# Feed-forward weight parts in three tiles by the order of their products, a fourth load buffer, and the order of loads in the merge

## The chip, the core and the metric

The kernel runs on one core of one Trainium2 chip. A core has TensorE (PE, matrix products), VectorE (DVE), ScalarE (ACT), GpSimd (POOL) and SyncE (SP), which here only issues transfers. The engines run their own instruction streams in order and wait for one another on semaphores. The metric is the device time of one execution in microseconds; the runs give a median.

## The reference, cut to what matters

Two layers of one trunk work on 512 latent and 128 context tokens of width 1024 (640 columns, called T). Each layer is: normalize, three token mixers A, B, C beside each other, a gated sum of their projections (the merge), one output projection, a residual add, normalize, a SwiGLU feed-forward part (FFN) of inner width 2816, a residual add.

```python
merged = g_a * (ya @ p['w_pa']) + g_b * (yb @ p['w_pb']) + g_c * (yc @ p['w_pc'])
...
mix, new_ctx = mixer_block(h, p, ctx, angs)          # returns merged @ p['w_out']
x = x + g1 * mix
h = rms_norm(x, p['norm2']) * (1 + sc2) + sh2
x = x + g2 * ((jax.nn.silu(h @ p['w_gate']) * (h @ p['w_up'])) @ p['w_down'])
```

## The kernel before

**Precision and layout.** Activations lie with features on the 128 partitions and tokens along the columns. A weight is loaded in f32 and split into two f16 tiles, a high part by ACT and a low part by DVE (`split`, L190; for other weights `wload`, L179). A product is then three f16 matmuls per row block of 128 (`mm3`): high by high, low by high, high by low, over 320 columns at a time.

**Who sets the order.** The program is written in data-flow order, and a scheduler puts the instructions of each engine into one static order. Blocks under `high_priority` are preferred, so loads move ahead as far as their buffers allow. A pool with `bufs=n` gives a tile's name n buffers in turn; an instruction that needs one waits for the last user of the old content. Everything that SP issues, gate tiles, branch weights, w_out, FFN weights, residual tiles (x) and modulation weights (wm), stands in one queue. `after` adds an ordering edge between two instructions of one engine without a semaphore.

**The merge** (`merge`, L1129). For each of eight feature blocks m it loads three tiles into `t3` (name mgt, three buffers): the gates of the branches (`d_gate`) or, where a branch was already projected and gated earlier, that result (`d_br`). With the branch weights (`w_br`, one product for m = 0 and two for each other m, each in two halves of 320 columns) PE fills PSUM (six banks, name g), DVE multiplies by the gate (mgt, L1149), POOL adds (mga), and ACT and DVE split the sum into mgh and mgl. Then w_out is loaded in eight blocks of 512 KB through two raw buffers (wf) and split into the eight buffers of the pool wo; three passes over the columns (320, 192, 128) make the output projection, the residual add and the sums of squares.

**The FFN** (`ffn`, L1266). Its three matrices are multiplied by a seven-product scheme on 2 x 2 blocks (Winograd's form of Strassen's). `norm_sums` makes the seven right-hand sides xs. `lhs` (L1201) makes the seven left-hand sides of a weight block: SP loads five sub-blocks of 256 columns into a tile wg (three buffers), POOL's queue adds a sixth onto two of them with an accumulating transfer, ACT and DVE split the three plain sub-blocks (`pw`, 768 columns), DVE adds one sum (L1212), POOL adds another (L1213), and ACT and DVE split the four sums (1024 columns). The seven results lie in one pair of tiles, pw0 and pw1, with five buffers; AT7 says where each product finds its part. `block` runs the products of a block in the order 1, 2, then 6, 5, 7, then 4, 3, and `run` interleaves them so that the 1, 2 of a block stand ahead of the 4, 3 of the block before. Intermediate products go from PSUM to SBUF by ACT copies (dp1, du2, du3, two buffers each). A block of the gate and up matrices has two calls of `lhs`, one of the down matrix one or two; there are 136 calls in the program. In layer 0 the FFN also computes the modulation of layer 1 (wm loads, products into at).

**Memory.** The scratch pool tmp (name sq, for squares) is open for the whole program.

Of the kernel before, what the change touches and what calls it, by code (L numbers as in the profile page):

```python
# [21 lines left out]
KD = 8  # L22
# [106 lines left out]

AT7 = {4: 0, 2: 1, 1: 2, 3: 3, 6: 4, 7: 5, 5: 6}  # L130

BT7 = {1: 0, 2: 1, 3: 2, 5: 3, 7: 4, 4: 5, 6: 6}
WGB = 3
PWB = 5


class Trunk:
    def __init__(self, tc, nc, a, o, ctx, dbg=None):
        self.tc, self.nc, self.a, self.o, self.dbg = tc, nc, a, o, dbg
        pool = lambda n, b, **k: ctx.enter_context(tc.tile_pool(name=n, bufs=b, **k))  # L140
        self.cp = pool("const", 1)
        self.tp = pool("tmp", 2)
        self.ctx = ctx
        self.xpool = None
        self.pspools, self.psn = ExitStack(), 0
        self.last_tanh = self.pending = None
        self.open_psum(at=2, md=1, g=4)
        self.dp = pool("scr", 1, space=DRAM)

    def pool(self, es, name, bufs=1, side=None):  # L150
        return es.enter_context(self.tc.tile_pool(name=name, bufs=bufs, side=side, reuse_waits="tile"))

    def open_x(self):
# [24 lines left out]

    def wload(self, src, n, pool=None, raw=None):  # L179
        nc = self.nc  # L180
        wf = self.sb(raw, [128, n], "wf") if raw else self.sb(self.wp, [128, n], "wf")
        wh = self.sb(pool or self.wq, [128, n], "wh", F16)
        wl = self.sb(pool or self.wq, [128, n], "wl", F16)
        with self.tc.high_priority():
            nc.sync.dma_start(wf, src)
            nc.scalar.activation(wh, wf, AF.Copy, scale=SW)  # L186
            nc.vector.scalar_tensor_tensor(wl, wf, SW, wh, op0=ALU.mult, op1=ALU.subtract)  # L187
        return wh, wl
# [35 lines left out]
    def after(self, i, j):  # L224

        info = mybir.DependencyInfo(mybir.DependencyClass.NoSync, mybir.DependencyReason.DATA)
        self.tc.add_manual_dep(i, j.name, info, reason="function tables")

# [900 lines left out]
    def merge(self, l, mp, wo, wr, mt, ys):  # L1129
        nc = self.nc  # L1130
        mgh = self.sb(mp, [128, KD, T], "mgh", F16)
        mgl = self.sb(mp, [128, KD, T], "mgl", F16)
        for m in range(KD):
            acc = self.sb(mp, [128, T], "mga", bufs=2)
            t3 = self.sb(mt, [128, 3, T], "mgt")
            late = [b for b in (0, 2, 1) if b == 1 or m >= EARLY[b // 2]]
            with self.tc.high_priority():
                for b in range(3):
                    nc.sync.dma_start(t3[:, b], self.d_gate[m, b] if b in late else self.d_br[m, b // 2])
                if late == [1]:  # L1140
                    nc.gpsimd.tensor_tensor(acc, t3[:, 0], t3[:, 2], op=ALU.add)
# [18 lines left out]
        for m in range(KD):  # L1160
            nc.sync.dma_start(self.x[:, m, :], self.xsrc[:, m, :])
            ws.append(self.wload(self.a["w_out"][l, m].rearrange("p k m -> p (k m)"), 1024, wo))
        for x0, x1 in COLS:
# [37 lines left out]
    def lhs(self, pool, src, n):  # L1201
# [4 lines left out]
        with self.tc.high_priority():  # L1206
            a = tile("wg", WGB, F32, 5)
            out = [tile(f"pw{i}", PWB, F16, 7) for i in range(2)]
            nc.sync.dma_start(a, src[:, 0:5])
            nc.gpsimd.dma_start(a[:, 3:5], src[:, 5:6].to_broadcast([128, 2, 128 * n]), accum_op=ALU.add)  # L1210
            self.split(out[0][:, 0:3], out[1][:, 0:3], a[:, 0:3], SW)
            nc.vector.tensor_tensor(a[:, 2], a[:, 4], a[:, 2], op=ALU.add)  # L1212
            nc.gpsimd.tensor_tensor(a[:, 1], a[:, 2], a[:, 1], op=ALU.add)  # L1213
            self.split(out[0][:, 3:7], out[1][:, 3:7], a[:, 1:5], SW)
        return {q: [[out[i][:, j, 128 * k:128 * k + 128] for k in range(n)] for i in range(2)] for q, j in AT7.items()}

    def block(self, pool, chunks, rhs, dst, done, urgent=False, after=None):
# [18 lines left out]

        def copy(p, tag):
            with first():
                t = self.sb(pool, [128, HT], tag, bufs=2)
                self.act(t, p, AF.Copy)  # L1240
                return t
        bank = lambda: self.psum("s")[:, :HT]
        a, b = bank(), bank()
        product(a, 1)
        p1 = copy(a, "dp1")
        product(b, 2)
        add(p1, b, 0)
        yield
        product(a, 6, True)
        u2 = copy(a, "du2")  # L1250
        b = bank()
        product(b, 5)
        product(a, 7, True)
        u3 = copy(a, "du3")
        add(u3, b, 3)
# [10 lines left out]
    def ffn(self, l, fs, ns):  # L1266
# [5 lines left out]
        ns.close()  # L1272
        wp = self.pool(fs, f"fw{l}")
        self.open_psum(s=7, at=1)
        d_x = self.sb(self.dp, [128, KD, T], f"d_x{l}")
# [142 lines left out]
    def layer(self, l):  # L1418
        tc = self.tc
        ys, ws, wfs = ExitStack(), ExitStack(), ExitStack()  # L1420
        self.yh, self.yl = [], []
        self.wp = self.pool(wfs, f"wf{l}", 2)
        self.wq = self.pool(ws, f"wst{l}", 3)
# [98 lines left out]
        with ExitStack() as es:  # L1522
            gp = self.pool(es, f"mg{l}")
            wo, mt = self.pool(es, f"wo{l}", 8), self.pool(es, f"mt{l}", MTB)
            self.merge(l, gp, wo, wr, mt, ys)
        wfs.close()
        with ExitStack() as es:
            self.ffn(l, es, ExitStack())
# [8 lines left out]
def layout(inp):  # L1537
# [45 lines left out]

    six = lambda w: np.stack([w[..., i, j, :, :] for i, j in ((1, 1), (0, 1), (0, 0), (0, 0), (1, 1), (1, 0))], -3)
    r["w_gu"] = six(gu).reshape(L, NF // 2, 2, 2, 128, 6, 256)
# [37 lines left out]
```

## Time and profile before

| | |
|---|---|
| median of 3 runs | 2754.21 us (2751.93 to 2755.40) |
| the profiled execution: its time, its span | 2747.09 us, 2745.2 us |
| PE busy | 2503.0 us (91%) |
| DVE busy | 1739.1 us (63%) |
| ACT busy | 1308.2 us (48%) |
| POOL busy | 941.4 us (34%) |
| mean granted clock of PE | 0.973 |
| moved by transfers | 434.44 MB |

The shares are means over stages with different limits. The stages are found in the timeline: the merge of layer 0 runs from 791.3 to 870.9 us, its output projection from there to about 925, its FFN from 939.1 to 1397.2; in layer 1 the merge begins at 2149.4 and the FFN lasts from 2297.6 to 2732.4.

### The profile page before, as it was taken

To read this page: it belongs to the slowest core of one execution; us is meant where nothing else is said; L and a number is where in the kernel's file an instruction comes from. 1 tells how busy PE (TensorE), PEld (TensorE's weight loads), DVE (VectorE), ACT (ScalarE), POOL (GpSimd) and SP (SyncE) were. 2 spreads that over 40 slices of the span, in tenths; PEclk is the share of its full clock that TensorE was granted. 3 is DMA by queue.
4 is the path that set the end of the run, shared out by engine and by line. 5 is a ranking of instruction groups with operands and counts; after the bars stand their busy time and mean duration, and the time that the engine had idled before them with its cause. 6 is when DMAs were issued, how large, how long until landed. Compare 5 with 4: busy or idle time off the path is not lost.

```text
span 2745.2 us, 53163 instructions
## 1 busy us (share of the span) xinstructions
PE 2503.0 (91%) x21022; PEld 1606.3 (59%) x21022; DVE 1739.1 (63%) x2984; ACT 1308.2 (48%) x2482; POOL 941.4 (34%) x876
## 2 busy tenths in 40 slices
PE   6999999999978899999889989999989788889896
PEld 3656666566336655656666666665753466566664
DVE  5639854325756677677787497432267657676877
ACT  5532754444642544344465345544545425444445
POOL 3252211211126355354433632022012455544544
PEclk9999999999999999999999999999999999999999
DMA  7787564436346187765543965534462641556563
GB/s 293 221 256 233 151 191 124 125 124 204 108 156 183 32 257 217 195 181 135 131 142 109 262 182 163 149 115 120 131 210 74 212 127 30 131 137 153 120 151 100
DMA packets 286395, 434.44 MB, mean 158 GB/s; under 512 B 112000, under 2 KB 192960, under 8 KB 286144
## 3 DMA queue, kind: packets, MB, share of 16 engines
q1 hardware_dynamic: 249152, 396.42, 46.5%
q0 software_dynamic: 36992, 34.61, 8.8%
q8 instruction: 165, 2.70, 0.4%
q14 instruction: 86, 0.70, 0.1%
HBM read 343.21 MB, written 73.92 MB: 152 GB/s over the span
## 4 chain that ended last, share of the span: by engine, by line
PE 44%; DVE 19%; DMA 18%; issue 6%; ACT 6%; POOL 5%; SPq 2%; POOLq 0%; DVEq 0%; ACTq 0%
PE f L199 11%; PE s L199 9%; PE g L199 7%; DMA wg<-in_w_gu 6%; PE ao L876 4%; DVE pw L193 4%; DMA wg<-in_w_down 2%; DVE z L675 2%; ACT pw L192 1%; DVE wl L187 1%; DVE zw L673 1%; POOL wg L1213 1%; DMA d_s<-sd 1%; DVE wg L1212 1%; PE at L980 1%
## 5 line engine op out<-in xcount | busy, mean ns | idle before, releaser
L199 PEld LDWEIGHTS <-pw 128*128 128x128 f16 x5544 | 539.7, 99 | 347.3 <-issue 55.5
L199 PEld LDWEIGHTS <-wh 128*128 128x128 f16 x4944 | 477.6, 99 | 211.5 <-issue 29.7
L199 PE MATMUL s<-xs,pw 128*128 128x320 f16 x3696 | 541.2, 304 | 47.2 <-ACT pw L192 13.3
L192 ACT ACTIVATE pw<-wg 128x1024 f16<-128x1024 f32 (+3 forms) x272 | 247.7, 923 | 251.4 <-POOL wg L1213 157.7
L193 DVE SCALAR_TENSOR_TENSOR pw<-wg,pw 128x1024 f16<-128x1024 f32 (+3 forms) x272 | 314.8, 1171 | 72.8 <-ACT pw L192 71.9
L199 PEld LDWEIGHTS <-wl 128*128 128x128 f16 x2472 | 244.5, 99 | 165.5 <-issue 76.3
L199 PE MATMUL s<-f,pw 128*128 128x320 f16 x1848 | 273.6, 303 | 35.6 <-ACT pw L192 17.1
L199 PE MATMUL f<-hh,wh 128*128 128x320 f16 x896 | 249.5, 300 | 0.1
L199 PE MATMUL f<-hh,wl 128*128 128x320 f16 x896 | 249.5, 300 | 0.0
L879 POOL TENSOR_TENSOR pacc<-pe,pacc 128x512 f32<-128x512 f32 x64 | 84.9, 1327 | 350.6 <-ACT pe L217 317.8
L199 PE MATMUL g<-hh,wh 128*128 128x320 f16 x704 | 201.7, 308 | 3.1 <-ACT sq L217 1.5
L199 PE MATMUL g<-hh,wl 128*128 128x320 f16 x704 | 201.5, 307 | 0.0
L1210 POOL DMA_DIRECT2D wg<-in_w_gu x88 | 105.6, 1205 | 218.9 <-DMA wg<-in_w_gu 120.3
L333 DVE SCALAR_TENSOR_TENSOR wl<-wf,wh 128x512 f16<-128x512 f32 x130 | 90.1, 720 | 142.7 <-ACT wh L217 142.6
L187 DVE SCALAR_TENSOR_TENSOR wl<-wf,wh 128x1024 f16<-128x1024 f32 (+4 forms) x116 | 126.7, 1097 | 36.9 <-ACT wh L186 36.6
L1213 POOL TENSOR_TENSOR wg<-wg 128x256 f32<-128x256 f32 (+1 forms) x136 | 125.0, 924 | 66.2 <-DVE wg L1212 63.8
L199 PE MATMUL f<-hl,wh 128*128 128x320 f16 x896 | 147.3, 299 | 0.0
L1212 DVE TENSOR_TENSOR wg<-wg 128x256 f32<-128x256 f32 (+1 forms) x136 | 91.8, 680 | 87.6 <-DMA wg<-in_w_gu 61.5
L186 ACT ACTIVATE wh<-wf 128x1024 f16<-128x1024 f32 (+4 forms) x116 | 96.0, 833 | 77.3 <-PE g L199 59.1
L217 ACT ACTIVATE pe<-at 128x512 f32<-128x512 f32 x128 | 75.1, 595 | 106.1 <-PE at L981 58.8
L818 POOL TENSOR_TENSOR rc<-rc,rot 128x512 f32<-128x512 f32 (+1 forms) x16 | 30.0, 1872 | 273.3 <-DVE rc L817 183.6
L199 PE MATMUL g<-hl,wh 128*128 128x320 f16 x704 | 114.6, 300 | 0.0
(370 smaller groups left out, 4805.3 us busy)
## 6 DMA issues: line engine op xcount, KB each, us to landing
wg<-in_w_gu SPq DMA_DIRECT2D x88, 640.0 KB, 4.9
wm<-in_w_mod SPq DMA_DIRECT2D x96, 512.0 KB, 5.3
wf<-in_w_in SPq DMA_DIRECT2D x112, 256.0 KB, 3.4
wg<-in_w_down SPq DMA_DIRECT2D x40, 640.0 KB, 4.1
wf<-in_w_in SPq DMA_DIRECT2D x44, 512.0 KB, 3.8
wg<-in_w_gu POOLq DMA_DIRECT2D x88, 256.0 KB, 4.6
d_s<-sd SPq DMA_DIRECT2D x20, 768.0 KB, 5.4
d_gate<-st SPq DMA_DIRECT2D x96, 160.0 KB, 2.7
```

Source lines behind the costliest of these rows:

```text
L186: nc.scalar.activation(wh, wf, AF.Copy, scale=SW)
L187: nc.vector.scalar_tensor_tensor(wl, wf, SW, wh, op0=ALU.mult, op1=ALU.subtract)
L192: nc.scalar.activation(hi, src, AF.Copy, scale=scale)
L193: nc.vector.scalar_tensor_tensor(lo, src, scale, hi, op0=ALU.mult, op1=ALU.subtract)
L199: mm = lambda *a, **k: nc.tensor.matmul(out, *a, skip_group_check=more, **k)
L217: i = self.nc.scalar.activation(out, in_, func, scale=scale, **kw)
L333: nc.vector.scalar_tensor_tensor(wl[:, sl], wf, SW, wh[:, sl], op0=ALU.mult, op1=ALU.subtract)
L876: nc.tensor.matmul(po[64 * j:64 * j + 64, :], vt(h, kt), es[j], start=n == 0, stop=n == 4)
L879: nc.gpsimd.tensor_tensor(acc[1], es[1], acc[1], op=ALU.add)
L1210: nc.gpsimd.dma_start(a[:, 3:5], src[:, 5:6].to_broadcast([128, 2, 128 * n]), accum_op=ALU.add)
L1212: nc.vector.tensor_tensor(a[:, 2], a[:, 4], a[:, 2], op=ALU.add)
L1213: nc.gpsimd.tensor_tensor(a[:, 1], a[:, 2], a[:, 1], op=ALU.add)
```

## The change

- **Order of loads in the merge.** `merge` keeps the last gate load of each m in `lds`. The w_out load of block m is ordered behind the gate loads of step m + 1 (the last two behind those of the last step), and the first four wg loads of the FFN behind the last gate load.
- **Weight parts in three tiles.** The sub-blocks are stored in another order (`six` and AT7), so that the accumulating transfer adds onto a[2:4]. Three pairs of tiles take the split parts: two sub-blocks (products 1 and 2), then, after DVE's sum, the three of products 6, 5 and 7, then, after POOL's sum, those of products 3 and 4. They have four, five and six buffers (PWB), in all as many bytes as before.
- **Buffers.** wg has four buffers. The copies dp1, du2 and du3 share one name with four buffers. tmp is closed before the FFN and opened anew in the next layer; the FFN has a pool of its own for sq.

```diff
-AT7 = {4: 0, 2: 1, 1: 2, 3: 3, 6: 4, 7: 5, 5: 6}
+AT7 = {2: (0, 0), 1: (0, 1), 6: (1, 0), 7: (1, 1), 5: (1, 2), 3: (2, 0), 4: (2, 1)}
...
-WGB = 3
-PWB = 5
+WGB = 4
+PWB = (4, 5, 6)
...
+    def open_tmp(self, l):
+        self.tp = self.pool(self.tmps, f"tmp{l}", 2)
...
-    def wload(self, src, n, pool=None, raw=None):
+    def wload(self, src, n, pool=None, raw=None, behind=None):
...
-            nc.sync.dma_start(wf, src)
+            ld = nc.sync.dma_start(wf, src)
+            if behind is not None:
+                self.after(ld.ins, behind)
...
+        lds = []
         for m in range(KD):
...
                 for b in range(3):
-                    nc.sync.dma_start(t3[:, b], self.d_gate[m, b] if b in late else self.d_br[m, b // 2])
+                    ld = nc.sync.dma_start(t3[:, b], self.d_gate[m, b] if b in late else self.d_br[m, b // 2])
+                lds.append(ld.ins)
...
-            ws.append(self.wload(self.a["w_out"][l, m].rearrange("p k m -> p (k m)"), 1024, wo))
+            ws.append(self.wload(self.a["w_out"][l, m].rearrange("p k m -> p (k m)"), 1024, wo, behind=lds[min(m + 1, KD - 1)]))
+        self.late = [lds[-1]] * WGB
...
             a = tile("wg", WGB, F32, 5)
-            out = [tile(f"pw{i}", PWB, F16, 7) for i in range(2)]
-            nc.sync.dma_start(a, src[:, 0:5])
-            nc.gpsimd.dma_start(a[:, 3:5], src[:, 5:6].to_broadcast([128, 2, 128 * n]), accum_op=ALU.add)
-            self.split(out[0][:, 0:3], out[1][:, 0:3], a[:, 0:3], SW)
-            nc.vector.tensor_tensor(a[:, 2], a[:, 4], a[:, 2], op=ALU.add)
-            nc.gpsimd.tensor_tensor(a[:, 1], a[:, 2], a[:, 1], op=ALU.add)
-            self.split(out[0][:, 3:7], out[1][:, 3:7], a[:, 1:5], SW)
+            ld = nc.sync.dma_start(a, src[:, 0:5])
+            if self.late:
+                self.after(ld.ins, self.late.pop())
+            nc.gpsimd.dma_start(a[:, 2:4], src[:, 5:6].to_broadcast([128, 2, 128 * n]), accum_op=ALU.add)
+            out = []
+
+            def parts(j, x):
+                out.append([tile(f"pw{j}{i}", PWB[j], F16, x.shape[1]) for i in range(2)])
+                self.split(out[j][0], out[j][1], x, SW)
+            parts(0, a[:, 0:2])
+            nc.vector.tensor_tensor(a[:, 1], a[:, 3], a[:, 1], op=ALU.add)
+            parts(1, a[:, 1:4])
+            nc.gpsimd.tensor_tensor(a[:, 0], a[:, 1], a[:, 0], op=ALU.add)
+            parts(2, a[:, 0:5:4])
...
-                t = self.sb(pool, [128, HT], tag, bufs=2)
+                t = self.sb(pool, [128, HT], "du", bufs=4)
...
         wp = self.pool(fs, f"fw{l}")
+        self.tp = self.pool(fs, f"sq{l}", 2)
...
+        if l:
+            self.open_tmp(l)
...
         wfs.close()
+        self.tmps.close()
...
-    six = lambda w: np.stack([w[..., i, j, :, :] for i, j in ((1, 1), (0, 1), (0, 0), (0, 0), (1, 1), (1, 0))], -3)
+    six = lambda w: np.stack([w[..., i, j, :, :] for i, j in ((0, 1), (0, 0), (0, 0), (1, 1), (1, 1), (1, 0))], -3)
```

## Rows read from the trace of the kernel before

**Rows 1.** Windows: stretch, us, busy us (count) of each engine, clock, DMA share, GB/s.

```profile
791.30:870.90 79.60, 58.13 (x398) 39.65 (x397) 58.80 (x74) 27.88 (x39) 47.95 (x44) 0.91 0.86 261
806.80:820.50 13.70, 5.27 (x20) 2.90 (x20) 8.80 (x15) 4.53 (x5) 3.50 (x3) 0.50 1.05 297
870.90:925.00 54.10, 50.75 (x553) 43.78 (x553) 23.68 (x45) 21.71 (x50) 20.23 (x30) 1.00 0.06 21
939.10:1397.20 458.10, 424.53 (x3112) 273.35 (x3111) 333.87 (x503) 204.47 (x330) 210.11 (x206) 0.98 0.67 178
992.00:1070.00 78.00, 72.06 (x569) 42.88 (x568) 55.03 (x71) 33.15 (x54) 41.42 (x40) 1.00 0.85 247
1223.30:1226.70 3.40, 3.40 (x15) 1.91 (x14) 2.76 (x5) 1.52 (x3) 0.86 (x1) 0.50 0.48 119
2297.60:2732.40 434.80, 391.97 (x2729) 266.56 (x2728) 320.57 (x476) 205.85 (x329) 209.28 (x206) 0.98 0.53 123
```

**Rows 2.** PE's waits in 785:872, layer 0's merge: us in total, times, longest.

```profile
PE g L199 <- DVE mgt L1149: 16.8, 7, 12.6
```

**Rows 3.** PE's waits in 2130:2240, layer 1's merge.

```profile
PE g L199 <- DVE mgt L1149: 17.4, 8, 12.4
```

**Rows 4.** Timeline of PE: start, us, engine, line, operation, [idle before, releaser].

```profile
815.23 0.42 PE L199 MATMUL g<-yh,wh 128*128 128x320 f16 x1 [12.58 <-DVE mgt L1149]
```

**Rows 5.** Timeline of SP, which issues the loads, in layer 0's merge.

```profile
796.17 0.37 SPq L1209 DMA_DIRECT2D wg<-in_w_gu  x1
...
799.51 1.59 SPq L185 DMA_DIRECT2D wf<-in_w_out  x2
801.14 4.17 SPq L1139 DMA_DIRECT2D mgt<-d_gate  x4
```

**Rows 6.** PE's waits in 940:1397, layer 0's feed-forward part.

```profile
PE s L199 <- ACT pw L192: 11.8, 10, 2.2
PE s L199 <- DVE pw L193: 7.7, 7, 3.3
PE s L199 <- ACT du L217: 5.7, 5, 3.6
```

**Rows 7.** PE's waits in 2298:2732, layer 1's feed-forward part.

```profile
PE s L199 <- ACT pw L192: 18.6, 18, 2.9
PE s L199 <- DVE pw L193: 12.4, 19, 1.6
```

**Rows 8.** The page's groups: count, busy us, mean ns, idle before, releasers.

```profile
L199 PE MATMUL s<-xs,pw 128*128 128x320 f16 x3696 | 541.2, 304 | 47.2 <-ACT pw L192 13.3
```

**Rows 9.** The page's DMA issues: count, KB each, us to landing.

```profile
wg<-in_w_gu SPq DMA_DIRECT2D x88, 640.0 KB, 4.9
...
wg<-in_w_gu POOLq DMA_DIRECT2D x88, 256.0 KB, 4.6
```

**Rows 10.** Timeline of SP in 990:1075: first and eleventh weight block.

```profile
992.02 0.33 SPq L1209 DMA_DIRECT2D wg<-in_w_gu  x1
...
1069.77 0.33 SPq L1209 DMA_DIRECT2D wg<-in_w_down  x1
```

**Rows 11.** Forms in 1000:1395 on DVE, on ACT; tile pw (min/median/max ns).

```profile
L193 DVE SCALAR_TENSOR_TENSOR pw<-wg,pw 128x1024 f16<-128x1024 f32 x53 | 69.4, 1315 | 23.3 <-ACT pw L192 23.0
L193 DVE SCALAR_TENSOR_TENSOR pw<-wg,pw 128x768 f16<-128x768 f32 x53 | 53.2, 1026 | 2.5 <-ACT pw L192 2.4
...
L193 DVE SCALAR_TENSOR_TENSOR pw<-wg,pw 128x512 f16<-128x512 f32 x4 | 3.7, 914 | 2.5 <-ACT pw L192 2.5
...
L192 ACT ACTIVATE pw<-wg 128x1024 f16<-128x1024 f32 x53 | 55.6, 1053 | 69.4 <-POOL wg L1213 69.0
...
L192 ACT ACTIVATE pw<-wg 128x512 f16<-128x512 f32 x4 | 2.5, 626 | 4.5 <-POOL wg L1213 4.5
...
L193 DVE SCALAR_TENSOR_TENSOR pw<-wg,pw x272: 546/1210/3508, 803.6 to 2720.3; 128x768 f16<-128x768 f32 x62, 128x1024 f16<-128x1024 f32 x62, 128x384 f16<-128x384 f32 x8, 128x512 f16<-128x512 f32 x4
```

**Rows 12.** SP's waits in 785:940.

```profile
SPq L304 <- DVE nts L1195: 73.2, 2, 71.3
```

More of the change, by code (lines that the diff above doesn't have):

```diff
@@ L141, in __init__ @@
         self.cp = pool("const", 1)
-        self.tp = pool("tmp", 2)
         self.ctx = ctx
+        self.tmps = ExitStack()
+        self.open_tmp(0)
         self.xpool = None
@@ L226, in after @@
         info = mybir.DependencyInfo(mybir.DependencyClass.NoSync, mybir.DependencyReason.DATA)
-        self.tc.add_manual_dep(i, j.name, info, reason="function tables")
+        self.tc.add_manual_dep(i, j.name, info, reason="order")
     def load_ln_exp(self):
@@ L1207, in lhs @@
             a = tile("wg", WGB, F32, 5)
-            out = [tile(f"pw{i}", PWB, F16, 7) for i in range(2)]
-            nc.sync.dma_start(a, src[:, 0:5])
-            nc.gpsimd.dma_start(a[:, 3:5], src[:, 5:6].to_broadcast([128, 2, 128 * n]), accum_op=ALU.add)
-            self.split(out[0][:, 0:3], out[1][:, 0:3], a[:, 0:3], SW)
-            nc.vector.tensor_tensor(a[:, 2], a[:, 4], a[:, 2], op=ALU.add)
-            nc.gpsimd.tensor_tensor(a[:, 1], a[:, 2], a[:, 1], op=ALU.add)
-            self.split(out[0][:, 3:7], out[1][:, 3:7], a[:, 1:5], SW)
-        return {q: [[out[i][:, j, 128 * k:128 * k + 128] for k in range(n)] for i in range(2)] for q, j in AT7.items()}
+            ld = nc.sync.dma_start(a, src[:, 0:5])
[11 more added lines that the diff above has]
+            parts(2, a[:, 0:5:4])
+        return {q: [[out[j][i][:, c, 128 * k:128 * k + 128] for k in range(n)] for i in range(2)] for q, (j, c) in AT7.items()}
     def block(self, pool, chunks, rhs, dst, done, urgent=False, after=None):
@@ L1235, in add, with copy @@
                 done(i, t)
-        def copy(p, tag):
+        def copy(p):
             with first():
-                t = self.sb(pool, [128, HT], tag, bufs=2)
+                t = self.sb(pool, [128, HT], "du", bufs=4)
                 self.act(t, p, AF.Copy)
@@ L1244, in block @@
         product(a, 1)
-        p1 = copy(a, "dp1")
+        p1 = copy(a)
         product(b, 2)
@@ L1249, in block @@
         product(a, 6, True)
-        u2 = copy(a, "du2")
+        u2 = copy(a)
         b = bank()
@@ L1253, in block @@
         product(a, 7, True)
-        u3 = copy(a, "du3")
+        u3 = copy(a)
         add(u3, b, 3)
```

## The prediction

> **What bounds the kernel now.** I read the windows by stage first [rows 1]. The reader is to see that TensorE (PE) sets the pace in the two stages that the change touches, the merge and the feed-forward part (FFN), but isn't full there. The FFN of layer 0 lasts 458.1 us with PE busy 424.53, that of layer 1 434.8 us with 391.97. The merge of layer 0 lasts 79.6 us with PE busy 58.13.
>
> The list of PE's waits says what ends the idle time. In the merges it is the gated sum: 16.8 us in the first [rows 2], 17.4 in the second [rows 3], and one wait of 12.6 and one of 12.4 hold most of it. The first ends at 815.23 [rows 4]. The SP timeline tells why [rows 5]: the gate tiles that VectorE (DVE) needs are issued from 801.14, after three FFN loads of 640 KB (the first at 796.17) and two w_out loads of 512 KB. None of those five is needed before the merge is over. The transfer engines are full then, share 1.05 at 297 GB/s, and after the wait PE runs at granted clock 0.50, the 1.2 GHz level [rows 1]. In the next stage, 870.9 to 925.0, the DMA share is 0.06: the same bytes would travel there for nothing.
>
> In the FFN the waits are for split weights (pw): 11.8 us that ScalarE (ACT) ends and 7.7 that DVE ends in layer 0, with 5.7 more for an ACT copy (du) that stands behind such splits [rows 6]; 18.6 and 12.4 in layer 1 [rows 7]. The ring of three load buffers (wg) explains them. I call one call of lhs a weight block; there are 136. Its load of 640 KB lands after 4.9 us and the accumulating one after 4.6 [rows 9]; sums and splits follow, and the buffer's next load may not start before the last split. A full block has 7 products x 2 row blocks x 3 matmuls = 42 matmuls at 541.2/3696 = 0.146 us [rows 8], 6.15 us of PE. From 992.02 to 1069.77 ten blocks are loaded [rows 10], one per 7.8 us: slower than PE takes them, though that stretch also holds modulation products.
>
> **The change, part by part.**
>
> *Gate loads first.* Nothing is removed; w_out and FFN loads move behind gate loads on SP's queue. Bytes up to the merge's end: 24 gate tiles of 320 KB, eight w_out of 512 KB and seven of the 15 branch weights of 256 KB (four raw and four split buffers hold the first eight), 13.9 MB. At the 297 GB/s of rows 1 that is 47 us. PE needs 30 half-products x 12 matmuls x 0.146 us, 52.6 us, so transfer can keep up. Upper bound of the gain: 16.8 + 17.4, and the half-clock stretch, whose 5.27 us of PE work would take 2.6 us less, in each merge: 39.4. Lower bound: nothing, if the transfer engines stay full. I take the two long waits and the clock, 12.6 + 12.4 + 5.2 = 30.2, leave the small waits, and charge 2 us per merge for w_out loads that now compete with gates, because 47 is near 52.6: **-26 us**.
>
> The new waits and their queue: w_out load m stands behind the gate loads of step m + 1, and these wait for one of three gate buffers, so branch weights queued behind them come late if a gate buffer does. That order of need is also PE's, so I add nothing. What is late next: the last w_out load is issued behind the last gate load, but its product comes eighth in the first pass, 7 x 24 x 0.146 = 25 us after the pass begins. FFN loads start at the latest at the merge's end, 870.9, and 68 us are left until the FFN's first long run at 939.1. Cover for their splits: from 870.9 to 925.0 DVE is busy 23.68 of 54.1 us and ACT 21.71. Four blocks need 4 x 2.85 = 11 us of DVE, so I cost them at nothing; if that cover is gone and they fall into the norm just ahead of 939.1, it is 11 us per layer, 22 in all.
>
> SP stands 71.3 us at a modulation load (wm) that waits for the norm's scratch [rows 12]. FFN loads five to eight must be issued ahead of it. They are ready when the first four buffers are split, so I charge nothing; if they stand behind it, layer 0 starts its FFN with four blocks of lead in place of eight, some 8 blocks x (7.8 - 6.15) = 13 us, once.
>
> *Four wg buffers, splits in three tiles.* With three buffers one round may take 3 x 6.15 = 18.5 us before PE waits, with four 24.6. A round without waits is 4.9 + 4.6 + 1.05 + 1.32 (the last splits, [rows 11]) = 11.9 us, and some 2 us for the two sums, an estimate; at 7.8 us a block it really took 23.4. So four buffers hold what three did not. The three tiles free the weights of products 1 and 2 early and let products 6, 5, 7 start without GpSimd's (POOL's) sum. What can go: 11.8 + 7.7 + 5.7 + 18.6 + 12.4 = 56.2 us of waits, and the half-clock stretches behind such waits. One is in rows 1 (1223.3: 3.40 us, all busy, at 0.50); there are seven in the two FFNs, 1.7 us lost in each, 11.9. Upper bound 68, lower bound nothing. I take 60%, **-41 us**, because from 992 to 1070 the DMA share is already 0.85 [rows 1], so layer 0 can't gain all.
>
> *More, shorter instructions.* Each block is split in pieces of 512, 768 and 512 columns instead of 768 and 1024. By the forms [rows 11] ACT takes 1053 ns for 1024 and 626 for 512, 0.83 ns a column and 0.2 us fixed: 0.2 x 136 = 27 us more work. DVE takes 1315, 1026 and 914 for 1024, 768 and 512: by the slope of the first two 0.16 us more per block, by the third row 0.91 + 1.03 + 0.91 - 1.03 - 1.32 = 0.5; 22 to 69 us in all. It is hidden as long as DVE has room: in the FFN it is busy 333.87 of 458.1 us, 73% [rows 1]. After POOL's sum only a 512 piece is left, 0.63 + 0.91 in place of 1.05 + 1.32, which shortens the round by 0.8 (in the gain above). I charge **+2 us**; the ends are nothing and 69 (rival C).
>
> The Trainium skill (Perfetto Trace Analysis, section Optimizing Scalar/DVE Operations) says both: grouping into larger operations helps when the engine is saturated, and breaking them up may let work complete sooner when the engine isn't saturated but causes bubbles on others. At 73% the trace fits the second clause and the sum above; by the first it would be rival C.
>
> *du in one tag of four buffers, tmp closed before the FFN, sq in the FFN's own pool.* These move memory only: three copies at most are alive in the four buffers. No instruction is added. Nothing, with a few us either way at the change of layers, where FFN tiles and the next layer's load buffers share addresses.
>
> **Sum.** -26 - 41 + 2 = -65 us. The profiled execution took 2747.09 us (span 2745.2, 1.9 around it), so 2682 in its frame; the median of the runs, 2754.21, is 7.1 above it, so **2689 us** for the median.
>
> **Rivals.**
> A. *The FFN stays as it is*: the fourth buffer fills, but the waits come from DVE and ACT taking their instructions in order, or from full transfers. For: DMA share 0.85 at 992 to 1070. Against: 0.53 over layer 1's FFN, which has the larger waits. -26 + 2: 2730 us.
> B. *The merge stays as it is*: the gates come first, but w_out loads take the place of the FFN loads and the wait splits into small ones. For: 47 against 52.6 us. Against: the three FFN loads in front of the gates are 1.97 MB, 6.6 us at 297 GB/s, and they do leave. -41 + 2: 2715 us.
> C. *Slower: the pieces make DVE the bound.* Place: each FFN weight block. Three pieces cost DVE 0.5 us more by the 914 row; if PE waits for each, 136 x 0.5 = 69 us, and no FFN wait goes. With the merge's 26: 2797 us. It decides from 26/136 = 0.19 us per block that PE really waits. For: one piece took 3508 ns against a median of 1210 [rows 11], so something holds DVE up at times. Against: 27% of DVE's time is idle. The Trainium skill (SBUF — State Buffer, section SBUF: two separate sides) tells of an exclusive lock: a DVE operation with two inputs in SBUF and a GpSimd operation that reads SBUF shut each other out for a whole instruction. By that rule POOL's sum, which now may run beside the second piece, would stretch it; the 3508 row agrees that pieces get stretched, not by what.
> D. *It doesn't do what it says*: the dependency only orders instructions on SP's queue, and if gate tiles wait for their own buffers as long as before, nothing moves: 2754 us. Against: the gates at 801.14 came right after the loads ahead of them [rows 5].
>
> **How the numbers follow.** Forecast 0.67, its own range 2657 to 2712 (the FFN gives 27 to 58, the merges 18 to 39). A 0.12, B 0.10, C 0.07, D 0.04. The range takes in the forecast, A and B: 2648 to 2736; it leaves out C, D and some edge of the forecast, under 2 in 10. Faster by over 0.2% (about what a measurement here can tell from no change): 0.67 + 0.12 + 0.10 = 0.89; same 0.04; slower 0.07.
>
> **What the profile after would show.** Merge right: gate rows come before w_out and FFN loads on SP, the wait for the gated sum is a few us per merge, and no clock of 0.50 follows; wrong: over 12 us of it per merge, or new PE waits for w_out's weights. FFN right: waits for pw below 25 us over both layers; wrong: they stay near 50. C shows as DVE over 85% busy in the FFN with pw waits that DVE ends. A late start shows as pw waits in the first 30 us of an FFN. The prediction would be wrong most likely through FFN waits that go from one engine's queue to another's.

## The result and the profile after

| | before | after |
|---|---|---|
| median of the runs timed together (4 each) | 2753.08 us (2751.93 to 2755.40) | 2772.32 us (2769.41 to 2780.06) |
| span of the profiled execution | 2745.2 us | 2767.6 us |
| PE busy | 2503.0 us (91%) | 2499.8 us (90%) |
| DVE busy | 1739.1 us (63%) | 1780.0 us (64%) |
| mean granted clock | 0.973 | 0.969 |

The change made the kernel slower: ratio 1.0073, 95% interval 1.0051 to 1.0096. The forecast was 2689 us.

Where the time went is read by stages, cut at marks in PE's timeline (first merge product, first product of the output projection, its last, the end of the FFN). us in the profiled executions:

| stage | before, layer 0 / 1 | after, layer 0 / 1 | difference |
|---|---|---|---|
| merge | 72.1 / 71.8 | 53.2 / 52.0 | -18.9 / -19.8 |
| output projection | 56.7 / 56.7 | 65.0 / 64.5 | +8.3 / +7.8 |
| norm and FFN | 475.3 / 452.6 | 520.9 / 470.8 | +45.6 / +18.2 |
| mixers of layer 1 | 754.1 | 738.4 | -15.7 |

What comes ahead of the first merge and behind the last FFN gives -3.2, and the whole is +22.4. So merge and output projection together gained 22.6 us, near the forecast; the norm and FFN, forecast at -39, lost 64. The mixers of layer 1, in which nothing was changed, took 15.7 us less, which the prediction has no term for. 10 of them are PE busy time (712.79 us in 1395.6:2149.4 before, 702.50 in 1427.8:2165.9 after) at a mean clock of 0.97 and 0.98; why is not shown. The windows of the changed kernel answer to [rows 1] (columns as there):

```profile
841.60:906.60 65.00, 56.16 (x577) 47.16 (x575) 39.21 (x62) 26.93 (x53) 37.98 (x43) 0.97 0.60 163
911.70:932.60 20.90, 8.10 (x49) 5.27 (x48) 20.17 (x40) 11.07 (x26) 10.97 (x18) 0.74 0.11 32
932.60:1427.50 494.90, 432.99 (x3109) 280.79 (x3109) 338.76 (x550) 208.09 (x385) 208.95 (x204) 0.95 0.62 162
992.00:1070.00 78.00, 66.92 (x512) 39.80 (x511) 50.75 (x74) 30.79 (x57) 35.64 (x34) 0.96 0.79 230
2308.40:2753.20 444.80, 393.86 (x2726) 271.44 (x2725) 342.99 (x529) 206.19 (x386) 211.61 (x204) 0.97 0.53 119
```

The third row is the FFN of layer 0 from its first long run of products. It has three matmuls fewer in the records than before, but PE is busy 8 us longer at a mean clock of 0.95 in place of 0.98, and idle 61.9 us in place of 33.6. DVE's share fell from 73% to 68%: its throughput isn't the bound. The second row is the end of the norm, 20.9 us in place of 14.2 (924.9 to 939.1 before); DVE is nearly full in both, 20.17 us busy after and 13.45 before.

SP's timeline in layer 0's merge answers to [rows 5]: gates go first, no wg load is among them, and the first comes at 849.74.

```profile
791.54 1.31 SPq L1146 DMA_DIRECT2D mgt<-d_br  x3
792.89 1.85 SPq L1146 DMA_DIRECT2D mgt<-d_gate  x4
794.79 1.52 SPq L189 DMA_DIRECT2D wf<-in_w_out  x1
...
849.74 0.33 SPq L1217 DMA_DIRECT2D wg<-in_w_gu  x1
```

PE's waits in 785:842, against [rows 2]:

```profile
PE g L205 <- DVE mgt L1157: 3.7, 3, 1.8
```

PE's waits in 925:1427, against [rows 6]:

```profile
PE s L205 <- ACT du L223: 26.7, 14, 5.3
PE at L312 <- DMA wm<-in_w_mod: 21.3, 10, 4.5
PE s L205 <- ACT xs L198: 12.8, 1, 12.8
```

and in 2290:2753, against [rows 7]:

```profile
PE s L205 <- ACT du L223: 16.5, 13, 3.7
PE s L205 <- DVE ff_s L1318: 14.3, 7, 3.3
PE s L205 <- ACT xs L198: 12.9, 1, 12.9
...
PE s L205 <- DVE pw L199: 0.7, 1, 0.7
```

The waits for split weights, 50.5 us in both layers before, are gone (one of 0.7 is left). In their place stand waits for the copies of intermediate products (du), for modulation weights (wm), for the right-hand sides (xs), and for DVE's own work on the products (ff_s and others, split weights left out: 42.3 us over both layers).

**One such wait, seen from both engines.** Timeline of PE, then of ACT, in 1228:1241 of the changed kernel (start, us, engine, line, operation, [idle before, releaser]):

```profile
1228.40 3.56 PE L205 MATMUL s<-xs,pw 128*128 128x320 f16 x25 [0.28 <-ACT du L223]
1237.29 4.16 PE L205 MATMUL s<-xs,pw 128*128 128x320 f16 x15 [5.34 <-ACT du L223]
```

```profile
1227.93 0.42 ACT L223 ACTIVATE du<-s 128x320 f32<-128x320 f32 x1
1234.98 0.47 ACT L198 ACTIVATE f<-ts 128x320 f16<-128x320 f32 x1 [6.64 <-POOL ts L1204]
1235.36 1.56 ACT L198 ACTIVATE pw<-wg 128x768 f16<-128x768 f32 x2
1236.83 0.74 ACT L223 ACTIVATE du<-s 128x320 f32<-128x320 f32 x2
```

PE's products are over at 1231.96. In ACT's order the two copies stand behind a conversion (f) that waits 6.64 us for POOL and behind both 768-column splits. They start 4.87 us after PE's products are over: 3.02 of that is the rest of the wait for POOL, 0.38 the conversion, 1.47 the two splits. So the splits themselves are the smaller part here. The next product of PE is accumulated onto the bank that the copy reads (`product(a, 6, True)` follows `copy(a)`), so PE stands for 5.34 us. What it costs besides is in the windows around it: the granted clock is 1.00 before the gap and 0.50, the 1.2 GHz level, behind it.

```profile
1228.40:1231.90 3.50, 3.50 (x25) 2.44 (x25) 2.88 (x4) 0.00 (x0) 2.31 (x2) 1.00 0.49 170
1237.30:1241.40 4.10, 4.10 (x16) 2.38 (x16) 4.10 (x7) 2.59 (x5) 1.45 (x1) 0.50 0.84 200
```

The Trainium skill (PSUM — Partial Sum Buffer, section Engine vs sequencer instructions) says that ScalarE's queue is strictly first in, first out; these rows agree, with copies whose inputs were ready at 1231.96 and which started at 1236.83.

### The profile page after: what moved, and what is told of

The parts are those of the page before. It is cut to its first block, busy times and chain, and to the rows that moved or that the text cites. A ratio compares the mean times of both kernels' runs of the same rounds, so it can differ in the third digit from the quotient of the medians.

```text
span 2767.6 us, 53522 instructions
## 1 busy us (share of the span) xinstructions
PE 2499.8 (90%) x21022; PEld 1616.9 (58%) x21022; DVE 1780.0 (64%) x3120; ACT 1320.0 (48%) x2618; POOL 941.9 (34%) x876
## 4 chain that ended last, share of the span: by engine, by line
PE 42%; DMA 23%; DVE 18%; issue 6%; ACT 5%; POOL 4%; SPq 1%; DVEq 0%; POOLq 0%; ACTq 0%
PE f L205 12%; DMA wg<-in_w_gu 11%; PE g L205 7%; PE ao L882 5%; PE s L205 5%; DMA wg<-in_w_down 5%; DVE pw L199 4%; POOL ts L1204 2%; DVE wl L193 2%; DVE z L681 1%; DMA wm<-in_w_mod 1%; DVE zw L679 1%; DVE wg L1227 1%; DMA sd<-d_kq 1%; PE at L1124 1%
## 5 line engine op out<-in xcount | busy, mean ns | idle before, releaser
L205 PEld LDWEIGHTS <-pw 128*128 128x128 f16 x5544 | 554.0, 101 | 382.6 <-issue 152.1
L205 PE MATMUL s<-xs,pw 128*128 128x320 f16 x3696 | 556.9, 311 | 83.7 <-ACT du L223 29.4
L199 DVE SCALAR_TENSOR_TENSOR pw<-wg,pw 128x512 f16<-128x512 f32 (+3 forms) x408 | 382.1, 954 | 75.9 <-ACT pw L198 75.6
L198 ACT ACTIVATE pw<-wg 128x512 f16<-128x512 f32 (+3 forms) x408 | 268.3, 680 | 244.0 <-PE s L205 112.1
L1220 POOL DMA_DIRECT2D wg<-in_w_gu x88 | 111.5, 1267 | 178.3 <-DMA wg<-in_w_gu 130.0
L1227 DVE TENSOR_TENSOR wg<-wg 128x256 f32<-128x256 f32 (+1 forms) x136 | 61.7, 455 | 136.7 <-DMA wg<-in_w_gu 91.9
```

The lines of the kernel that those rows point to most:

```text
L198: nc.scalar.activation(hi, src, AF.Copy, scale=scale)
L199: nc.vector.scalar_tensor_tensor(lo, src, scale, hi, op0=ALU.mult, op1=ALU.subtract)
L205: mm = lambda *a, **k: nc.tensor.matmul(out, *a, skip_group_check=more, **k)
L1220: nc.gpsimd.dma_start(a[:, 2:4], src[:, 5:6].to_broadcast([128, 2, 128 * n]), accum_op=ALU.add)
L1227: nc.vector.tensor_tensor(a[:, 1], a[:, 3], a[:, 1], op=ALU.add)
```

## The experiments

Each run's ratio is to the kernel before on the same chip in the same hour (its medians there: 2757.91 for e1 to e4, 2755.97 for e5 to e8, 2753.55 for e9 to e11, 2759.60 for e12 and e13). Runs without an interval have a single time. Columns: whether the merge's loads go in the new order, wg buffers, pieces of a block's splits, and the names of the copies with their buffers (preferred: written as early as the splits are).

| run | order of loads | load buffers | pieces | names of copies | median us | ratio (95%) |
|---|---|---|---|---|---|---|
| e1_order_alone | new | 3 | 2 | 3 of 2 | 2718.88 | 0.9865 (0.9841 to 0.9888) |
| e2_ffn_alone | old | 4 | 3 | 1 of 4 | 2769.17 | 1.0036 (1.0019 to 1.0052) |
| e3_du_six | new | 4 | 3 | 3 of 2 | 2699.65 | |
| e4_two_pieces | new | 4 | 2 | 1 of 4 | 2705.59 | |
| e5_ring_of_six | new | 4 | 3 | 1 of 6 | 2767.74 | |
| e6_copies_ahead | new | 4 | 3 | 1 of 4, preferred | 2725.24 | 0.9896 (0.9876 to 0.9915) |
| e7_three_load_buffers | new | 3 | 3 | 3 of 2 | 2757.44 | 1.0001 (0.9985 to 1.0017) |
| e8_du_six_timed | new | 4 | 3 | 3 of 2 | 2696.64 | 0.9789 (0.9773 to 0.9805) |
| e9_two_pieces_du_six | new | 4 | 2 | 3 of 2 | 2702.52 | 0.9815 (0.9787 to 0.9842) |
| e10_six_and_ahead | new | 4 | 3 | 3 of 2, preferred | 2684.32 | 0.9744 (0.9727 to 0.9760) |
| e11_pieces_alone | old | 3 | 3 | 3 of 2 | 2772.49 | 1.0061 (1.0042 to 1.0080) |
| e12_norm_cover | new | 4 | 3 | 3 of 2, preferred | 2678.86 | 0.9710 (0.9682 to 0.9738) |
| e13_ahead_one_ring_of_six | new | 4 | 3 | 1 of 6, preferred | 2716.39 | |

**e1: the order of loads alone**, on the kernel before.

```diff
+ lds.append(ld.ins)
...
+ ws.append(self.wload(..., wo, behind=lds[min(m + 1, KD - 1)]))
+ self.late = [lds[-1]] * WGB
```

> The kernel before with the load order alone: w_out loads and the first three FFN loads behind gate loads; splits, buffers and memory as before. Theory 1 (the FFN's new splits and buffers lose the time, by work that stands in ACT's order in front of the copies PE waits for): the merges give their 39 us, the output projections lose some 16, the FFNs stay within 10 us of before: about 2735 us. Theory 2 (the late FFN loads lose the time): FFNs some 50 us longer as after, about 2775 us.

Measured 2718.88 us, 39 less than before. The merges are 53.9 and 51.8 us, and the output projections 64.8 and 65.3. So the merge's mechanism is right, and the prediction set both its sizes too small: gain 30 against 38, price 4 against 17. Together that is 21 us. The other part of the 39 lies elsewhere: by the profiled executions (2745.2 and 2717.4 us) the mixers of layer 1 are 13 us shorter and the norm and FFN of layer 0 some 8 longer, and the kernel before was profiled in an execution faster than its median (2747.09 against 2754.21). Theory 1 expected 2735.

**e2: all but the order of loads.** The changed kernel without the two ordering edges.

```diff
-            ws.append(self.wload(..., wo, behind=lds[min(m + 1, KD - 1)]))
+            ws.append(self.wload(..., wo))
-        self.late = [lds[-1]] * WGB
+        self.late = []
```

> The changed kernel without any of the new order edges: splits in three tiles, four load buffers, du, tmp and sq as changed. Theory 1: merges as before (72 us each), both FFNs longer by 45 and 18 us as in the changed kernel: about 2795 us. Theory 2: FFNs shorter than before, about 2710 us.

2769.17 us, under the 2795 of theory 1 and far above the 2710 of theory 2: the loss is in the FFN's part. Its merges last 55.4 and 55.2 us though, 2 to 3 us longer than with the edges, and not the 72 that theory 1 expected. SP's timeline in 788:850 shows w_out loads between the gates again, but no FFN load until 848.62:

```profile
791.45 2.65 SPq L189 DMA_DIRECT2D wf<-in_w_out  x2
795.80 1.29 SPq L1146 DMA_DIRECT2D mgt<-d_br  x3
797.13 0.43 SPq L1146 DMA_DIRECT2D mgt<-d_gate  x1
...
848.62 1.43 SPq L1217 DMA_DIRECT2D wg<-in_w_gu  x3
```

With tmp closed and a fourth load buffer the FFN's loads come late even without the edges. PE's waits for the gated sum stay small (3.0 us in 785:845) with w_out loads among the gates, and in e11, where FFN loads stand among them again, they are 30.8 us over both merges. So it was the FFN loads, rather than those of w_out, that the merge waited behind. (What holds them back in e2 was not tried.)

**e3: copies in three names again**, the rest as changed.

```diff
-                t = self.sb(pool, [128, HT], "du", bufs=4)
+                t = self.sb(pool, [128, HT], tag, bufs=2)
```

> The changed kernel with the copies back in three names of two buffers each. Theory 1a (the one ring of four copies binds: a copy waits for an older one and PE for the copy): waits of PE for du fall from 43 us to about 10, time about 2735 us. Theory 1b (the three pieces on ACT, not the ring): waits for du stay near 40 us, time within 10 us of 2772.

2699.65 us: this one line holds 73 us. But neither theory's signs hold together: the time moved as in theory 1a, further than expected, and the waits for du stayed at 41.1 us, as in theory 1b. So the sum of these waits is not what the time follows; e6 comes back to this. Without the line the change is within 11 us of the forecast, partly by luck: by the stages of e8, the same kernel, merges and projections give -23, the norm and FFN -15 in place of -39, and the rest, which the sum left out, -9.

**e4: two pieces again**, copies in one name of four.

```diff
-PWB = (4, 5, 6)
+PWB = 5
...
-            parts(0, a[:, 0:2])
...
-            parts(1, a[:, 1:4])
...
-            parts(2, a[:, 0:5:4])
+            self.split(out[0][:, 0:3], out[1][:, 0:3], a[:, 0:3], SW)
...
+            self.split(out[0][:, 3:7], out[1][:, 3:7], a[:, 1:5], SW)
```

> The changed kernel with the weight split as before (one pair of tiles, five buffers, pieces of 768 and 1024 columns), but four load buffers, the new order of loads and the new memory. Theory 1b: waits for du fall to about 10 us, waits for pw come back in part, time about 2725 us. Theory 1a: waits for du stay near 40 us. Theory 2: about 2770 us.

2705.59 us; waits for du fall to 16.3 us and waits for pw come back at 32.1, as in theory 1b, 19 us faster than it expected. Either part alone does no harm beside four load buffers (table at e9); with both the kernel is 67 us slower than with the ring alone and 73 slower than with the pieces alone (e3).

**e5: six buffers in the one name.**

```diff
-                t = self.sb(pool, [128, HT], "du", bufs=4)
+                t = self.sb(pool, [128, HT], "du", bufs=6)
```

> The changed kernel, but the one ring of copies back (du) has six buffers in place of four. The written order of every engine inside both feed-forward parts is the changed kernel's, line for line; only the merge and the output projection differ, by where the first load buffers come to lie. Theory R (a copy waits for one of four buffers): the copies come free with six, and the time falls to that of the run with three names of two, about 2700 us. Theory O (ScalarE's order is what delays the copies: both 768-column splits stand ahead of a pair of copies, and one name, however many buffers it has, gives that order): the waits for du stay at 30 to 45 us and the time at 2760 to 2775 us.

2767.74 us, du waits of 43.7 us as after's 43.2: theory O. It isn't the number of buffers. What differs between one name and three is the order that the scheduler writes, for ACT among others. From the instruction streams, over both FFNs: how often two or more copies stand together behind both 768-column splits, with no copy between the splits.

```
changed kernel 56     e5 56     e6 2     e13 2
e3, e8          5     e10 2     e12 3    e7  4     e11 5
```

By ACT's rows in the traces, e2 has 56 too. With two pieces the count is 26 in the kernel before and in e1, 15 in e9 and 12 in e4: one name raises it only beside three pieces, which fits the table at e9. The count marks an order and is no price by itself, since 26 of them stand beside du waits of only 8.9 us in the kernel before.

**e6: copies preferred** in the changed kernel (one ring of four, three pieces).

```diff
-            with first():
+            with self.tc.high_priority(10 ** 5):
                 t = self.sb(pool, [128, HT], "du", bufs=4)
```

> The changed kernel, ring of four and three pieces kept; the copies back are preferred in the order as the splits are, so that a copy stands between the two 768-column splits or ahead of them in place of both copies behind both splits. Theory O (order on ScalarE): the stretches of half clock behind the copies go and the time falls by 50 to 75 us, to 2695 to 2720 us. Theory R (the ring of four): copies still wait for buffers, 2760 to 2775 us. Theory P (the pieces as such cost DVE and ACT time): also no change. In between would mean that the preferred copies delay splits that PE then waits for (pw waits above 20 us).

2725.24 us, 47 less than the changed kernel, no buffer added: theory O, but short of its range; the pw waits that it named for that case don't come. PE's waits for du halve (20.6 against 43.2 us); DVE's ff_s stays (second line).

```profile
PE s L205 <- ACT du L223: 20.6, 20, 2.8
...
PE s L205 <- DVE ff_s L1318: 14.9, 10, 3.7
```

That line points at a second engine. The waits of the FFN's products that DVE ends (split weights left out) are 42.3 us in the changed kernel, 46.2 in e5 and 39.3 in e6, but 5.1 in e8 and 14.2 in e10, which have three names; du waits alone are 39.5 us in e8, hardly less than the 43.2 of the changed kernel. DVE's order holds such cases too. In 1140:1152 of the changed kernel PE stands 2.70 us for a residual add (x) that reads its bank; the add stands on DVE behind a weight sum that waits 6.75 us for its load (DVE's timeline, then PE's):

```profile
1149.79 0.42 DVE L1227 TENSOR_TENSOR wg<-wg 128x256 f32<-128x256 f32 x1 [6.75 <-DMA wg<-in_w_gu]
1150.13 0.54 DVE L1194 SCALAR_TENSOR_TENSOR x<-s,mod,x 128x320 f32<-128x320 f32 x1
```

```profile
1150.73 1.49 PE L205 MATMUL s<-xs,pw 128*128 128x320 f16 x5 [2.70 <-DVE x L1194]
```

Over layer 0's FFN DVE's idle time before these sums is 80.5 us in the changed kernel (932:1428), 46.0 in e6 (930:1389) and 2.5 in e8 (930:1375); the groups of the first and the last, shapes kept apart:

```profile
L1227 DVE TENSOR_TENSOR wg<-wg 128x256 f32<-128x256 f32 x57 | 25.3, 443 | 80.5 <-DMA wg<-in_w_gu 53.9 <-DMA wg<-in_w_down 26.5
L1227 DVE TENSOR_TENSOR wg<-wg 128x256 f32<-128x256 f32 x57 | 33.8, 596 | 2.5 <-DMA wg<-in_w_gu 2.3
```

So the order of one name costs on ACT and on DVE, and e6 mends mostly the first. How the 75.7 us divide between the two was not tried.

**e7: three load buffers**, else e3.

```diff
-WGB = 4
+WGB = 3
```

> The run with the copies in three names of two buffers (e3_du_six), but with three load buffers (wg) in place of four: one part of the change undone. The prediction's theory (a round of three buffers is too short, the fourth holds what three did not): waits for split weights come back, slower than the four-buffer version by 15 to 40 us, 2715 to 2740. Rival: the loads run ahead by themselves once the first pieces free their products early, and the waits that are left are ScalarE's order, so the time is that of e3 within 5 us, about 2700.

2757.44 us, 61 more than e8; the fourth buffer is worth more than expected. But no wait for split weights comes back. PE waits 67.6 us for du (40 times). Pairs behind two 768-column splits are not to blame this time (4 in the count above); ACT's timeline in 1255:1268 shows one of these waits:

```profile
1261.81 0.84 ACT L198 ACTIVATE pw<-wg 128x768 f16<-128x768 f32 x1 [2.15 <-DVE wg L1227]
1263.46 0.63 ACT L198 ACTIVATE pw<-wg 128x512 f16<-128x512 f32 x1 [0.80 <-POOL wg L1229]
1264.61 0.63 ACT L198 ACTIVATE pw<-wg 128x512 f16<-128x512 f32 x1 [0.52 <-POOL wg L1229]
1265.15 0.42 ACT L223 ACTIVATE du<-s 128x320 f32<-128x320 f32 x1
```

The splits are waited for one by one on ACT, since the loads are late, and the copy stands behind them; PE's gap there is 3.57 us. A late load shows as a wait for a copy.

**e8: e3, timed**, with the edit of e3.

> The kernel of e3_du_six once more, now timed in rounds beside the others: 2695 to 2705 us and a ratio of 0.978 to 0.982 to the kernel before if its one look was typical. The reference for e6 and e7 on the same chip.

2696.64 us. The FFN of layer 0, 930.9 to 1374.7, beside the third row of after's windows:

```profile
930.90:1374.70 443.80, 413.93 (x3109) 273.50 (x3109) 349.37 (x551) 213.03 (x386) 210.97 (x204) 0.98 0.69 181
```

Of the 51 us between the two, 19 are PE busy with the same 3109 matmuls (432.99 against 413.93, clock 0.95 and 0.98), and 32 are idle (61.9 against 29.9). In this layer the waits for du halve (26.7 against 13.3 us); in layer 1 they rise (16.5 against 26.2), and there it is the waits that DVE ends that go.

**e9: two pieces and three names**, the edits of e3 and e4 together.

> The changed kernel with both doubtful parts undone: splits in one pair of tiles as before (768 and 1024 columns) and copies back in three names of two buffers. What is left of the change is the order of loads, the fourth load buffer and the moved scratch memory. Theory O (three pieces help as long as the order on ScalarE lets a copy through between them): slower than e8_du_six_timed by 5 to 15 us, 2702 to 2712. Rival (three pieces only cost work, 0.2 us on ScalarE and 0.2 to 0.5 on VectorE per block): as fast or faster, 2680 to 2697.

2702.52 us, 6 more than e8, at the edge of theory O's range; the intervals overlap, so three pieces are not shown to gain anything by themselves. With e1, e4, e8 and the changed kernel this completes the table of the two parts, at four load buffers:

| | three names of two | one name of four |
|---|---|---|
| two pieces | 2702.5 | 2705.6 |
| three pieces | 2696.6 | 2772.3 |

**e10: copies preferred, three names**, on e8.

```diff
-            with first():
+            with self.tc.high_priority(10 ** 5):
                 t = self.sb(pool, [128, HT], tag, bufs=2)
```

> e8_du_six_timed with the copies back preferred in the order as well, as in e6. Theory O: the waits for du (39.5 us in e8) halve as in e6 and the time falls to 2675 to 2690. Rival (what order can give is taken already by the three names; the copies that move up only push splits back): within 0.3% of e8, 2690 to 2705.

2684.32 us: theory O by the time; du waits are 28.9 us, none over 2.3, which is a quarter less and not half. In 1160:1172 of its trace ACT waits for POOL too, for 4.11 us, but only one split is left between that and the copy:

```profile
1167.70 0.47 ACT L198 ACTIVATE f<-ts 128x320 f16<-128x320 f32 x1 [4.11 <-POOL ts L1204]
1168.08 0.83 ACT L198 ACTIVATE pw<-wg 128x768 f16<-128x768 f32 x1
1168.81 0.42 ACT L223 ACTIVATE du<-s 128x320 f32<-128x320 f32 x1
```

PE's gap at that copy is 0.43 us, also because the wait for POOL ends before PE's products do (1167.70 and 1168.28).

**e11: three pieces alone**, on the kernel before: `lhs`, `six` and AT7 as changed, with

```diff
-PWB = 5
+PWB = (4, 5, 6)
 WGB = 3
```

> The kernel before with one part of the change alone: splits in three pieces into three pairs of tiles. Three load buffers, three names of copies, loads in the merge and scratch memory stay as they were. Theory Q (with three load buffers, splits that are preferred and in three pieces stand on ScalarE waiting for their loads with the copies behind them): slower than before by 25 to 50 us, 2780 to 2805, with du waits above 50 us, which is the loss that e7 shows against e1 (2757 against 2719). The prediction's theory (short pieces free their products early and cost 2 us): 2735 to 2758. Theory P (VectorE has too little room): slower too, but with pw waits that VectorE ends.

2772.49 us: slower by 0.6%, du waits 65.7 us, none for pw: theory Q, although below its 2780. With three load buffers shorter pieces lose; e7 and e11 agree on why.

**e12: splits of blocks five to eight held behind the norm**, on e10. `xend` are ACT's and DVE's last instructions for xs.

```diff
+                if held:
+                    self.after(i[0], self.xend[0])
...
+            if held:
+                self.after(ad.ins, self.xend[1])
```

> e10_six_and_ahead, but ScalarE's splits and VectorE's sums of weight blocks five to eight of each layer are ordered behind the last right-hand side (xs) of the norm. Theory N (splits that fall into the norm make it longer, a part that the prediction priced at 11 us per layer if the cover is gone and charged at nothing): the wait for xs of 12.8 us per layer falls to about 6, and the time by 8 to 16 us, 2668 to 2677. Rival (what is held back is late for the first products): waits for pw or wm at the start of the feed-forward part take the gain, 2680 to 2690.

2678.86 us, ratio 0.9710, the fastest version here, 2 us outside theory N's range. The wait for xs falls from 12.8 to 5.0 us in layer 0 (PE's timeline in 905:925):

```profile
922.85 2.29 PE L206 MATMUL s<-xs,pw 128*128 128x320 f16 x8 [5.03 <-ACT xs L198]
```

The stage of norm and FFN is 7.5 and 7.0 us shorter than in e10 (theory N, in its place), yet the runs gain only 5.5: the mixers of layer 1, in which nothing was changed, take 753.4 us in place of 739.4. 12 of these 14 us are PE busy time (712.90 against 701.05) at a mean clock of 0.97 and 0.98; the instructions there stand in another order too, but that this is the reason is not shown.

**e13: e6 with six buffers.**

```diff
-                t = self.sb(pool, [128, HT], "du", bufs=4)
+                t = self.sb(pool, [128, HT], "du", bufs=6)
```

> e6_copies_ahead with six buffers in the one ring of copies. In the feed-forward parts the written order of every engine is that of e6, so that only buffers differ; e10 has six buffers too, in three names, and another order. Theory O (order alone): the time stays at 2717 to 2732 as in e6 and the 41 us between e6 and e10 are order. Theory R (with the copies moved up, four buffers hold them): 2680 to 2700 as e10.

2716.39 us, 1 us under theory O's range and far from theory R's. The single time is 9 us below e6, but by the traces norm and FFN of both layers together are 3 us longer than in e6, so nothing shows that six buffers gain there; what is shorter in the trace are the projections (5 us) and the mixers of layer 1 (6). The 41 us between e6 and e10 go with the names, that is with the order.

## Why the prediction was wrong, point by point

- **The step that failed** is "du in one tag of four buffers ... These move memory only ... Nothing, with a few us either way". The premise holds, four buffers do suffice (e5), but the conclusion doesn't: a tile's name takes part in the written order. With one name beside three pieces the engines got an order in which, on ACT, pairs of copies stand behind both 768-column splits, and PE accumulates onto the bank that they read; on DVE, work that PE waits for stands behind weight sums whose loads are late. It cost 75.7 us (2772.32 less e8's 2696.64), idle time and half clock. e6, which changes the preference of the copies alone, gives 47 of it back and leaves DVE's part. That the name decides, and not the number of buffers, is shown (e5, e8); how much each engine's order costs is not, and why the scheduler orders one name otherwise than three stays open.
- **Four wg buffers and three tiles, -41 + 2.** With the names kept, norm and FFN take 15 us less than before by the stages of e8, and e8 stands 22 us below e1: about half of the forecast. Only with edits that the change did not have does it come near, 35 with the copies preferred (e10) and 40 with the norm held free (e12). So this term was set too large as well: it let 60% of the waits that it named go and put nothing in their place. Its reasons were half right. The working compares a round of 23.4 us, taken at the pace with the waits in it, with what four buffers allow, so it doesn't show that the loads set that pace. The fourth buffer does gain: with two pieces 16 us (e9 against e1, which differ in the scratch memory too), with three 61 (e8 against e7). The three pieces gain nothing that can be told with four buffers and lose 39 with three (e7 against e1, which holds the moved scratch memory too). The pw waits went, as forecast, and by the sign that the prediction set (below 25 us) the FFN would be right; but what was late next was the copy on ACT and the work on DVE, the case that the prediction named as its likeliest failure without pricing it. The moved scratch memory was not tried alone.
- **Gate loads first, -26.** The two merges gained 38.7 us by the stages, not 30: small waits and clock went too. In the output projection, where 2 us per merge were charged, 8 went: w_out splits and the first FFN splits now fall there, DVE busy 39.21 us in place of 21.47 in the same stage before (863.4 to 920.0; the merge of [rows 1] takes in the first 7.5 us of the projection), with a wait of 5.1 us for sqacc. Net -22.6 against -26, right for partly wrong sizes, and so in part luck.
- **Cover ahead of the FFN, nothing.** The other case of that sentence came true: splits fell into the norm, DVE was busy 20.17 of its last 20.9 us, and the wait for xs is 12.8 and 12.9 us against 7.5 and 5.3 before. The prediction priced it at 22 us for both layers; by e12 it is 14.5. But the late loads, from which that passage starts, don't do it: with them and two pieces the wait for xs is 12.5 us for both layers (e1) and 12.6 (e9), with the old order of loads and three pieces 24.7 (e11). It goes with the three pieces.
- **SP at the modulation load, nothing or 13 us.** The first value held: SP issues nine FFN loads, from 849.74 on, ahead of the first modulation load at 933.13, and stands 6.1 us for the norm's scratch (785:940) in place of 73.2. Later in that FFN PE waits 21.3 us for wm in place of 4.7 (e8: 14.1, e1: 8.6). That is another wait, for which the prediction had no term.
- **Rivals.** A and B: no, the FFN moved and so did the merges; but A named the mechanism, waits from DVE and ACT taking their instructions in order, with a size of nothing. C had the sign, at twice the size, but not the cause: 0.7 us of pw waits that DVE ends, DVE at 68%, and e8 has the same three pieces without the loss. The Trainium skill's second clause (Perfetto Trace Analysis, section Optimizing Scalar/DVE Operations), that shorter instructions may let work complete sooner where an engine isn't saturated, is borne out neither way with four buffers (6 us, within the intervals); with three buffers the runs go against it (e11, 0.6% slower). The lock of rival C was not tried. D: no.

## What to carry to other kernels

Where an engine takes its instructions in order and also serves the accumulating engine with short copies, price a rearrangement by what will stand ahead of those copies, and by what that in turn waits for, not by its own duration: here one name cost 75.7 us, more than the rest of the change gained. An edit that "moves memory only" can rewrite the order of every engine, so compare the instruction streams of both kernels before costing it at nothing. When a wait is removed, read which wait the same engine's next instruction will end.

## What the runs showed of the hardware and the program that was not expected

- A gap of 5.34 us on PE was followed by granted clock 0.50 for the 4.1 us after it; between e8 and the changed kernel such stretches made the same 3109 matmuls 19 us longer, against 32 us of plain idle time.
- The same late loads show as waits for pw with two pieces (e1: 32.7 us that ACT ends, 22.1 that DVE ends) and as waits for du with three (e7: 67.6 us, no pw row): the name in the list of waits follows the order on the engines, not the cause. The sum of one such row can mislead too: du waits of 43.2 and 39.5 us stand in kernels 75.7 us apart.
- Stages that no edit touched moved by up to 15.7 us, most of it PE busy at another mean clock, more than several of the terms in the sum.
